# First units on the unnormalized input, weight sums on VectorE, and a longer load time in the scheduler: two layers of a hybrid decoder trunk

## The chip, the cores and the metric

The kernel runs on one core of one Trainium2 chip. The metric is device microseconds (us) of one execution. Engines are named as the profile names them: PE (TensorE; PEld is its weight load), DVE (VectorE), ACT (ScalarE), POOL (GpSimd), SP (the engine that issues most transfers).

## The reference

One sequence of 1024 positions, width 1024, two layers, all in f32. Each layer is a mixer and a squared-ReLU MLP, both behind an RMSNorm whose result is scaled and shifted by columns computed from a conditioning vector c. Here is what matters of it:

```python
mod = c_act @ ada_w[layer] + ada_b[layer]          # c_act = silu(c); 6 x 1024 columns
sh_m, sc_m, gt_m, sh_f, sc_f, gt_f = jnp.split(mod, 6, axis=-1)
h = rmsnorm(x, norm_mix_w[layer]) * (1 + sc_m) + sh_m
y = even_mixer(h, ...) if layer % 2 == 0 else odd_mixer(h, ...)
x = x + gt_m * y
h = rmsnorm(x, norm_mlp_w[layer]) * (1 + sc_f) + sh_f
x = x + gt_f * (jnp.square(jax.nn.relu(h @ w1)) @ w2)
# at the end: rmsnorm(x, final_norm_w)

# even_mixer: proj = h @ w_in, split into xr, yr, q, k, v, g (8 heads' worth of columns);
# xr: causal depthwise conv of width 4, then a gated linear recurrence (RG-LRU) times gelu(yr);
# q, k, v: rotary, chunkwise retention, group norm, times silu(g); both concatenated @ w_out
```

## The kernel before, in words

**Arithmetic.** Activations lie with features on the 128 partitions and half of the sequence, f = 0 or 1, in 512 columns. A dense product of two f32 matrices is made as three products of parts: each factor is split into a high part (a rounded copy, made by ACT) and a low part (the rest, made by a subtraction, mostly on DVE), and hi·hi, hi·lo and lo·hi are added up in PSUM (`mm3`). A *unit* is one 128-column block of a weight matrix: it takes 24 matmuls of 128x512 for each half, 48 in all. `operand` splits an activation, `split` a raw weight (loaded by SP as 512 KB into a `raw` slot).

**Order.** The program doesn't run in the order of its text. A `Recorder` collects every operation with an assumed duration, and `place()` schedules them all by simulation: of the operations that are ready, an engine takes the one with the smallest priority, which is its place in the text plus a bias (`with bias(...)`; BIG is larger than the program, LATER is 300 places). Slots come from pools: `heap` (73 slots of 128x512), `raw` (4), `w` (6), `pad` (4), and in PSUM `dps` (3) and `psum` (5). For a transfer the simulation adds bytes/380 ns to the time at which the transfers before it are through, and then 2000 ns until it has landed. What comes out is a fixed order for each engine and each queue; on the chip, every engine runs its list in that order and waits with semaphores.

**Start.** `csil`, the silu of c on all partitions, and `ccol`, the same as columns, come first. For each of 8 chunks j of the width, the shift `mod[:, j]` is a product on PE of `ada0[j]` with `ccol` (stationary a column of `ccol`, moving 128 columns of `ada0`, which gives a row that ACT copies and PE transposes to a column), and the scale `mod[:, 8+j]` is made by DVE from `ada[j]` and `csil`, and becomes `wsc[:, j]`. x's half 0 is loaded, its inverse root mean square `rs0` found by PE column sums (`rstd_half`), x multiplied by it (`scaled`), and `first_operand` makes the operand `x*rs0*wsc + mod`. Half 1 follows, its seven sums of squares on POOL. The first LEAD = 3 units then run together: their matmuls for f = 0, then those for f = 1 (f = 1 into the pool `psum`). Before, these are x0, x1 and q0 in `EVEN_ORDER` (x: input of the recurrence, y its gate, q, k, v, g of the retention); the low parts of their weights are made on POOL. `lru_in`, through `pad_in`, takes an x unit out of PSUM and convolves it.

**Then** 24 units of the even mixer in all, 16 units of the output projection (`out_proj`, whose 8 results per half are each added to x on DVE; after the last of a half a column sum on PE opens the norm), the MLP of layer 0, odd mixer, output projection, MLP of layer 1, final norm. Both products of an MLP are made by Strassen's scheme in Winograd's form: seven products P1 to P7 for each of 16 groups, 112 *steps* of 12 matmuls in the up half and 112 in the down half. Its weight operands need sums of blocks of the raw weights. Some are made by the transfer itself (`dma_add`: an accumulating transfer issued by POOL), two per group in each half by POOL's `tensor_tensor`: in the up half `x += P1` and `P2 += x` (`up_factor`), in the down half `a11 += x` and `a12 += a11` (`down_factor`); 128 over both layers. `W_LOADS` gives the step of the down half at which each weight block is asked for. `ada_some` asks for 512 KB of scale or gate weights that DVE multiplies with `csil` (tile names `raw<-raw,blk`); in the down half of layer 0 it is called at every fourth step. `last_adds` puts the last products of the down half into x.

## Time and profile before

| | us |
|---|---|
| median of 3 executions | 2349.3 |
| lowest and highest | 2345.51, 2351.92 |
| the profiled execution's own time | 2352.24 |
| its span | 2350.5 |
| mean granted TensorE clock, share of full speed | 0.991 |

The span is the time from the first to the last record of the profiled execution; 1.7 us of its own time lie around it. The profile is of one execution, so its rows add up to its own time, which is 3 us above the median. The kernel has about these stages: the start to 79 us, even mixer and output projection to 412, up half of layer 0 to 788, its down half to 1090, odd mixer and its output projection behind that, the same two halves for layer 1, and the final norm up to 2350.

### The profile page before, as it was taken

The numbers are of one execution on the slowest core, as the hardware profiler recorded it, in microseconds if no ns is written. First come the engines' busy times: TensorE is split into PE (matmuls) and PEld (weight loads), VectorE is DVE, ScalarE is ACT, GpSimd is POOL, SyncE is SP. The second block draws the span as 40 slices with busy tenths as digits, with TensorE's granted clock in tenths as the row PEclk, the third lists the DMA queues.
The fourth block names the chain that finished last, engine by engine and source line by source line (L and its number), as shares of the span: only waits on it lengthen the run. The fifth ranks groups of instructions, "written<-read, shape, count | busy, mean of one in ns | idle before, by whom it ended". The sixth has DMA issues, their size and how long they took to land.

```text
span 2350.5 us, 31521 instructions
## 1 busy us (share of the span) xinstructions
PE 2285.3 (97%) x10906; PEld 1871.1 (80%) x10906; DVE 1701.7 (72%) x2702; ACT 1275.0 (54%) x2377; POOL 513.5 (22%) x602
## 2 busy tenths in 40 slices
PE   7999999899999999999999999999999999999998
PEld 4787888678878778887787887888878888788886
DVE  7997667896555786887976687566687555676776
ACT  6787453565545544445755574656465555544444
POOL 3000000022221230500073426430022222140500
PEclk9999999999999999999999999999999999999999
DMA  8253338757664997753212122244358665896752
GB/s 290 90 135 117 117 120 283 246 157 219 192 180 156 311 346 244 211 189 117 73 39 77 48 57 68 59 141 141 128 154 238 194 188 159 265 312 193 185 161 94
DMA packets 199076, 393.35 MB, mean 167 GB/s; under 512 B 30146, under 2 KB 40962, under 8 KB 198916
## 3 DMA queue, kind: packets, MB, share of 16 engines
q1 hardware_dynamic: 180484, 357.78, 45.5%
q0 software_dynamic: 18432, 33.56, 8.8%
q8 instruction: 85, 1.39, 0.2%
q14 instruction: 75, 0.61, 0.1%
HBM read 308.91 MB, written 82.35 MB: 166 GB/s over the span
## 4 chain that ended last, share of the span: by engine, by line
PE 73%; issue 7%; DMA 7%; DVE 6%; ACT 5%; POOL 1%; SPq 0%; POOLq 0%; DVEq 0%; ACTq 0%
PE dps L342 39%; PE psum L342 35%; ACT heap L342 4%; DVE heap L342 4%; DMA raw<-in_dram 3%; DMA heap<-in_dram 1%; DMA h_spill<-heap 1%; DVE w L342 1%; ACT w L342 1%; POOL pad L342 1%; DVE raw L342 1%; DMA heap<-h_spill 1%; POOL raw L342 0%; POOL heap L342 0%; ACT L342 0%
## 5 line engine op out<-in xcount | busy, mean ns | idle before, releaser
L342 PE MATMUL dps<-heap,w 128*128 128x512 f32 x5016 | 1246.2, 396 | 14.9 <-DVE heap L342 8.7
L342 PEld LDWEIGHTS dps<-heap,w 128*128 128x128 f32 x5016 | 928.0, 189 | 211.0 <-ACT heap L342 10.6
L342 PE MATMUL psum<-heap,w 128*128 128x512 f32 x3816 | 899.7, 392 | 14.7 <-DVE blk L342 5.8
L342 PEld LDWEIGHTS psum<-heap,w 128*128 128x128 f32 x3816 | 718.9, 189 | 173.2 <-ACT heap L342 10.1
L342 ACT ACTIVATE heap<-heap 128x512 f32<-128x512 f32 (+2 forms) x1055 | 619.9, 609 | 258.6 <-DVE heap L342 200.5
L342 DVE TENSOR_TENSOR heap<-heap,heap 128x512 f32<-128x512 f32 (+1 forms) x799 | 580.2, 750 | 79.9 <-ACT heap L342 75.1
L342 ACT ACTIVATE w<-heap 128x512 fp32r<-128x512 f32 x224 | 140.6, 630 | 276.3 <-PE psum L342 219.9
L342 ACT ACTIVATE w<-raw 128x512 fp32r<-128x512 f32 (+1 forms) x248 | 192.2, 778 | 175.0 <-PE dps L342 93.6
L342 DVE TENSOR_TENSOR w<-raw,w 128x512 fp32r<-128x512 f32 (+1 forms) x213 | 192.9, 910 | 75.1 <-ACT w L342 69.6
L342 DVE TENSOR_TENSOR w<-heap,w 128x512 fp32r<-128x512 f32 x192 | 159.5, 836 | 97.1 <-ACT w L342 96.6
L342 POOL DMA_DIRECT2D raw<-in_dram x32 | 27.9, 873 | 718.5 <-DMA x_spill<-heap 297.3
L342 POOL TENSOR_TENSOR blk<-blk,blk 32x31 f32<-32x31 f32 (+15 forms) x248 | 173.9, 701 | 38.6 <-DMA blk<-n_full 11.5
L342 POOL TENSOR_TENSOR heap<-heap,heap 128x512 f32<-128x512 f32 x74 | 114.4, 1557 | 201.6 <-ACT heap L342 103.5
L342 ACT ACTIVATE heap<-psum 128x512 f32<-128x512 f32 (+6 forms) x189 | 89.3, 480 | 81.3 <-PE psum L342 80.4
L342 PE MATMUL psum<-heap,heap 128*128 128x128 f32 (+4 forms) x1064 | 130.5, 264 | 2.5 <-DVE heap L342 2.2
L342 PEld LDWEIGHTS psum<-heap,heap 128*128 128x128 f32 (+2 forms) x1064 | 113.1, 169 | 23.6 <-DVE heap L342 5.0
L342 DVE SCALAR_TENSOR_TENSOR raw<-raw,blk 128x1024 f32<-128x1024 f32 x80 | 98.8, 1237 | 30.2 <-DMA raw<-in_dram 29.8
L342 POOL DMA_DIRECT2D heap<-in_dram x64 | 59.8, 979 | 268.9 <-DVE heap L342 137.4
L342 DVE TENSOR_TENSOR w<-pad,w 128x512 fp32r<-128x512 f32 x64 | 58.3, 910 | 75.3 <-ACT w L342 75.2
L342 ACT ACTIVATE w<-pad 128x512 fp32r<-128x512 f32 x64 | 40.4, 632 | 126.0 <-POOL pad L342 71.4
L342 DVE TENSOR_TENSOR heap<-psum,heap 128x512 f32<-128x512 f32 x89 | 61.0, 686 | 48.2 <-PE psum L342 39.5
L342 ACT ACTIVATE heap<-dps 128x512 f32<-128x512 f32 (+1 forms) x134 | 77.5, 585 | 24.0 <-PE dps L342 13.7
(180 smaller groups left out, 1384.8 us busy)
## 6 DMA issues: line engine op xcount, KB each, us to landing
raw<-in_dram SPq DMA_DIRECT2D x232, 512.0 KB, 4.1
heap<-in_dram SPq DMA_DIRECT2D x226, 256.0 KB, 5.6
h_spill<-heap SPq DMA_DIRECT2D x224, 256.0 KB, 4.4
heap<-h_spill SPq DMA_DIRECT2D x224, 256.0 KB, 5.2
heap<-in_dram POOLq DMA_DIRECT2D x64, 256.0 KB, 6.8
x_spill<-heap SPq DMA_DIRECT2D x48, 256.0 KB, 3.1
heap<-x_spill SPq DMA_DIRECT2D x48, 256.0 KB, 5.4
pad<-in_dram SPq DMA_DIRECT2D x32, 256.0 KB, 2.5
```

The source lines that it names most:

```text
L342: op.call(*a, **k)
```

## The change

Five parts.

1. **Scheduler.** The transfer rate goes from 380 to 360 bytes per ns, and the time until a transfer has landed from 2000 ns to 3500 (issued by SP) or 5500 (issued by POOL). These numbers are only used to choose the order.
2. **Start.** x's half 0 is loaded chunk by chunk, each followed by its two scale weights. The operand of the lead units for f = 0 becomes `plain`, the split of x*wsc, without `rs0` and without the shift. What is missing is put in where the unit leaves PSUM: `pad_in` multiplies by `rs0` (a product along the columns) and adds `lead_bias`, a column per unit: the product of its raw weights with the shift, 24 matmuls with a single moving column, for which the three raw weights are held. The lead units become x0, x1, x2, which all leave through `pad_in`. f = 1 and all later units use the full operand as before. The shift is made with `ada0` as stationary factor and one column of `ccol` as moving one, which gives a column directly. The lead weights' low parts, and half 1's seven sums, go from POOL to DVE.
3. **Weight sums.** The 128 sums go from POOL to DVE.
4. **Loads of the MLP.** `W_LOADS`: in the down half x is asked for 8 steps earlier, a12 one, a21 six, a22 two. The scale and gate loads in the down half of layer 0 go from steps 2, 6, 10, ... to every third step from step 34 on.
5. `last_adds` gets the bias LATER.

The core of the diff:

```diff
-                    dma_free = max(dma_free, now) + op.bytes / 380.0
-                    op.end = dma_free + 2000.0
+                    dma_free = max(dma_free, now) + op.bytes / 360.0
+                    op.end = dma_free + (5500.0 if e == "POOL" else 3500.0)
...
-              "x0 x1 l2 q0 k0 v0 x2 x3 l2 q1 k1 v1 y0 y1 q2 k2 v2 y2 q3 k3 v3 y3 g0 g1 g2 g3".split()]
+              "x0 x1 x2 l2 q0 k0 v0 x3 l2 q1 k1 v1 y0 y1 q2 k2 v2 y2 q3 k3 v3 y3 g0 g1 g2 g3".split()]
...
-W_LOADS = {(i + n * j, name): j for i, n, name in ((-8, 1, "a11"), (0, 1, "a12"), (1, 2, "x"), (10, 2, "a21"), (24, 1, "a22"))
+W_LOADS = {(i + n * j, name): j for i, n, name in ((-8, 1, "a11"), (-7, 2, "x"), (-1, 1, "a12"), (4, 2, "a21"), (22, 1, "a22"))
...
-            split(hi, lo, raw, (), G if i < LEAD else V)
+            split(hi, lo, raw)
+            if i < LEAD:
+                lead_raw.append(raw)
...
             if kind == "P6":
-                G.tensor_tensor(pw["x"], pw["x"], pw["P1"], ALU.add)
+                V.tensor_tensor(pw["x"], pw["x"], pw["P1"], ALU.add)
...
         def last_adds(f, ks):
-            for k in ks:
-                add_to(f, k, shared[k % 4], f == 1 and k < 4)
+            with bias(LATER):
+                for k in ks:
+                    add_to(f, k, shared[k % 4], f == 1 and k < 4)
...
-            if l == 0 and n % 4 == 2:
+            if l == 0 and n >= 32 and n % 3 == 1:
                 ada_some(1, [marks[-1]])
...
+    plain = []
     for j in range(KC):
+        xh[0].append(ht("x"))
+        dma(xh[0][j], xT[j, :, 0:HT])
+        if 0 < j <= LEAD:
+            with bias(2 * BIG):
+                push()
...
+        w = wsc[:, j:j + 1]
+        V.scalar_tensor_tensor(w, mod[:, 8 + j:9 + j], 1.0, cc("nmix", j), ALU.add, ALU.mult)
+        hi, lo = hsplit_tiles()
+        act(hi, xh[0][j], AF.Copy, scale=w)
+        V.scalar_tensor_tensor(lo, xh[0][j], w, hi.bitcast(F32), ALU.mult, ALU.subtract)
+        plain.append((hi, lo))
+    xh[1] = load_half(xT, 1)
+    scaled(1, rstd_half(xh[1]))
+    rs0 = rstd_half(xh[0])
+    hh = [[], []]
+    pb = pmt()
+    for j in range(KC):
+        for q in range(2):
+            a = ht("ada")
+            dma(a, ada0[j][:, q * HT:(q + 1) * HT])
+            for k in range(4):
+                T.matmul(pb[:, j:j + 1], a[:, k * P:(k + 1) * P], ccol[:, 4 * q + k:4 * q + k + 1],
+                         start=(q == 0 and k == 0), stop=(q == 1 and k == 3))
+        V.tensor_tensor(mod[:, j:j + 1], pb[:, j:j + 1], cc("ada_b", j), ALU.add)
+        hh[1].append(first_operand(1, j))
+    lead_bias = small("lead_bias", [LEAD])
+    for u, raw in enumerate(lead_raw):
+        for k in range(KC):
+            T.matmul(pb[:, 8 + u:9 + u], raw[:, k * P:(k + 1) * P], mod[:, k:k + 1], start=(k == 0), stop=(k == KC - 1))
+    V.tensor_copy(lead_bias, pb[:, 8:8 + LEAD])
+    scaled(0, rs0)
+    for j in range(KC):
+        hh[0].append(first_operand(0, j))
...
     def pad_in(key, f, ps, b=None):
-        act(raw[:, 3:], ps, AF.Copy)
+        if b is None:
+            act(raw[:, 3:], ps, AF.Copy)
+        else:
+            V.tensor_tensor(raw[:, 3:], ps, rs0, ALU.mult)
+            act(raw[:, 3:], raw[:, 3:], AF.Identity, bias=b)
...
-    first = dense(hh, LEAD, pmt)
+    first = dense([plain, hh[1]], LEAD, pmt)
```

How the scheduler places it, at three places. Each row is an instruction: the helper's line, the operation, out<-in by tile names (pool and number), its shape, and how many alike follow each other.

**PE at the start of the program**, right behind the eight products that make `csil`. Before (`ccol` is the stationary column of the shift, `ones_r` the column sum of squares, `ident` the transpose of the row):

```order
L342 MATMUL psum_305<-s_301,ones_f 128x128
L342 MATMUL psum_334<-heap_168,ccol 1x128 x4
L342 MATMUL psum_334<-heap_170,ccol 1x128 x4
L342 MATMUL psum_349<-heap_340,ones_r 128x512
L342 MATMUL psum_334<-ident,s_351 128x1
L342 MATMUL psum_349<-heap_345,ones_r 128x512
L342 MATMUL psum_361<-heap_178,ccol 1x128 x4
L342 MATMUL psum_361<-heap_180,ccol 1x128 x4
L342 MATMUL psum_383<-heap_186,ccol 1x128
L342 MATMUL psum_361<-ident,s_379 128x1
L342 MATMUL psum_383<-heap_186,ccol 1x128 x3
L342 MATMUL psum_383<-heap_188,ccol 1x128 x4
L342 MATMUL dps_404<-heap_398,w_331 128x512
```

After:

```order
L342 MATMUL psum_301<-s_298,ones_f 128x128
L342 MATMUL dps_338<-heap_332,w_314 128x512
L342 MATMUL dps_342<-heap_332,w_325 128x512
L342 MATMUL dps_338<-heap_344,w_314 128x512
L342 MATMUL dps_338<-heap_332,w_319 128x512
L342 MATMUL dps_338<-heap_336,w_314 128x512
L342 MATMUL dps_338<-heap_346,w_314 128x512
L342 MATMUL dps_338<-heap_336,w_319 128x512
L342 MATMUL dps_342<-heap_344,w_325 128x512
```

The shift products, the column sum and the transposes stood ahead of the first dense matmul (`dps<-heap,w`); now the dense matmuls of the lead units follow at once.

**PE at the end of the first half of the output projection of layer 0.** The dense rows are units of half f = 1, and `psum<-heap,ones_r` is the column sum for f = 0, which waits for the last addition to x. Before:

```order
L342 MATMUL dps_3777<-heap_3404,w_3690 128x512
L342 MATMUL dps_3777<-heap_3306,w_3707 128x512
L342 MATMUL dps_3777<-heap_3392,w_3690 128x512
L342 MATMUL dps_3777<-heap_3479,w_3690 128x512
L342 MATMUL psum_3816<-heap_3804,ones_r 128x512
L342 MATMUL dps_3777<-heap_3392,w_3707 128x512
L342 MATMUL dps_3777<-heap_3494,w_3690 128x512
L342 MATMUL dps_3777<-heap_3506,w_3690 128x512
L342 MATMUL psum_3816<-heap_3811,ones_r 128x512
```

After:

```order
L342 MATMUL dps_3840<-heap_3284,w_3771 128x512
L342 MATMUL dps_3840<-heap_3330,w_3771 128x512
L342 MATMUL dps_3840<-heap_3284,w_3781 128x512
L342 MATMUL psum_3847<-heap_3835,ones_r 128x512
L342 MATMUL dps_3840<-heap_3297,w_3771 128x512
L342 MATMUL dps_3840<-heap_3343,w_3771 128x512
L342 MATMUL dps_3840<-heap_3297,w_3781 128x512
L342 MATMUL dps_3840<-heap_3301,w_3771 128x512
L342 MATMUL dps_3840<-heap_3381,w_3771 128x512
L342 MATMUL dps_3840<-heap_3301,w_3781 128x512
L342 MATMUL dps_3840<-heap_3310,w_3771 128x512
L342 MATMUL dps_3840<-heap_3387,w_3771 128x512
```

Before, 20 dense matmuls stand between the last unit of f = 0 and the first column sum; after, 27, and the second column sum follows 12 rows behind the first in place of 3.

**The weight sums at the start of the up half of layer 0.** Before, on POOL, between the issues of transfers (`DMA`; `pad` holds x, `raw` holds P1 and P2):

```order
L342 DMA pad_1697<-in_dram 128x512
L342 DMA raw_4145<-in_dram 128x512
L342 TENSOR_TENSOR pad_1395<-pad_1395,raw_4139 128x512
L342 DMA raw_4245<-in_dram 128x512
L342 TENSOR_TENSOR raw_4139<-raw_4139,pad_1395 128x512
L342 DMA pad_4312<-in_dram 128x512
L342 TENSOR_TENSOR pad_1485<-pad_1485,raw_4234 128x512
```

After, on DVE, between the operand splits (`w<-pad,w` is the low part of a weight factor, `heap<-heap,wsc,heap` the norm's product for an activation):

```order
L342 TENSOR_TENSOR w_4260<-raw_4219,w_4260 128x512
L342 SCALAR_TENSOR_TENSOR heap_4281<-heap_3457,wsc,heap_4265 128x512
L342 TENSOR_TENSOR w_4278<-pad_1332,w_4278 128x512
L342 SCALAR_TENSOR_TENSOR heap_4292<-heap_3466,wsc,heap_4265 128x512
L342 TENSOR_TENSOR pad_1332<-pad_1332,raw_4166 128x512
L342 SCALAR_TENSOR_TENSOR heap_4302<-heap_3459,wsc,heap_4265 128x512
L342 TENSOR_TENSOR raw_4166<-raw_4166,pad_1332 128x512
L342 TENSOR_TENSOR w_4304<-pad_1332,w_4304 128x512
```

Both sums now stand in DVE's order, in which a wait for their inputs holds back what stands behind them.

## Rows read from the trace of the kernel before

**Rows 1.** The profile page, part 1: busy time of each engine, its share of the span, and its instructions.

```profile
PE 2285.3 (97%) x10906; PEld 1871.1 (80%) x10906; DVE 1701.7 (72%) x2702; ACT 1275.0 (54%) x2377; POOL 513.5 (22%) x602
```

**Rows 2.** The timeline of PE, at eight places. Columns: start and length in us, engine, line, operation, out<-in, partitions by columns, shape, count; in brackets the idle time just before it and what released it. Nearly everything runs through one helper line, so the line says nothing here.

```profile
419.65 0.79 PE L342 MATMUL psum<-heap,ones_r 128*128 128x512 f32 x1 [7.44 <-ACT heap L342]
...
494.87 0.80 PE L342 MATMUL psum<-heap,w 128*128 128x512 f32 x1 [2.08 <-ACT heap L342]
...
531.38 2.79 PE L342 MATMUL psum<-heap,w 128*128 128x512 f32 x11 [1.42 <-ACT heap L342]
...
804.83 1.58 PE L342 MATMUL psum<-heap,w 128*128 128x512 f32 x4 [2.88 <-DVE blk L342]
...
839.57 2.93 PE L342 MATMUL dps<-heap,w 128*128 128x512 f32 x6 [2.61 <-DVE heap L342]
...
1744.27 0.96 PE L342 MATMUL psum<-heap,w 128*128 128x512 f32 x3 [1.38 <-DVE heap L342]
...
1777.36 2.81 PE L342 MATMUL psum<-heap,w 128*128 128x512 f32 x11 [1.09 <-ACT heap L342]
...
2050.25 3.35 PE L342 MATMUL psum<-heap,w 128*128 128x512 f32 x9 [2.74 <-DVE blk L342]
```

**Rows 3.** Busy time in windows: the stretch in us, its length, then for PE, PE's weight loads, DVE, ACT and POOL the busy us with (instructions), the granted TensorE clock as a share of full speed, the DMA share and GB/s.

```profile
50.00:100.00 50.00, 49.17 (x206) 37.45 (x204) 46.99 (x102) 39.24 (x63) 0.00 (x0) 1.00 0.22 72
...
150.00:200.00 50.00, 48.31 (x241) 39.38 (x240) 44.19 (x77) 42.41 (x82) 1.74 (x2) 1.00 0.46 127
...
200.00:250.00 50.00, 49.58 (x257) 41.39 (x256) 35.70 (x77) 26.30 (x71) 0.00 (x0) 1.00 0.37 116
...
420.00:425.00 5.00, 5.00 (x16) 3.95 (x16) 3.94 (x7) 2.79 (x4) 0.00 (x0) 0.69 0.90 290
...
495.00:500.00 5.00, 4.65 (x10) 3.21 (x11) 5.00 (x9) 3.04 (x5) 0.88 (x1) 0.50 0.47 90
```

**Rows 4.** The timeline of PE from 55 to 90 us: the first matmuls of the lead units' second half, and the fourth unit's 42 first ones (they write to the pool dps).

```profile
60.69 0.84 PE L342 MATMUL psum<-heap,w 128*128 128x512 f32 x3
...
78.97 9.68 PE L342 MATMUL dps<-heap,w 128*128 128x512 f32 x42
```

**Rows 5.** The timeline of DVE (first three) and of POOL, which is GpSimd (last two), from 0 to 65 us.

```profile
6.26 1.66 DVE L342 TENSOR_SCALAR s<-ident,ccol 128x128 f32<-128x128 f32 x8
...
28.96 1.70 DVE L342 SCALAR_TENSOR_TENSOR heap<-heap,blk 128x512 f32<-128x512 f32 x1
...
55.76 8.57 DVE L342 TENSOR_TENSOR heap<-heap,heap 128x512 f32<-128x512 f32 x14 [1.14 <-ACT heap L342]
...
13.53 2.46 POOL L342 TENSOR_TENSOR w<-raw,w 128x1024 fp32r<-128x1024 f32 x1 [11.66 <-ACT w L342]
...
28.54 11.46 POOL L342 TENSOR_TENSOR heap<-heap,heap 128x512 f32<-128x512 f32 x7 [1.93 <-ACT heap L342]
```

**Rows 6.** The DMA view from 0 to 60 us: GB/s in 40 slices of 1.5 us.

```profile
GB/s 0 145 269 276 272 333 421 395 399 404 388 389 386 400 393 393 373 386 391 378 382 385 385 384 388 386 389 374 244 69 109 295 391 364 21 5 11 0 0 0
```

**Rows 7.** PE's instructions grouped by line and form: shapes, count, then busy us, mean ns of one (the ends of pipelined ones overlap, so busy divided by count is the pace), and the idle time before them.

```profile
L342 PE MATMUL psum<-heap,ccol 128*1 128x128 f32 x128 | 17.9, 293 | 5.7 <-DMA heap<-in_dram 5.7
...
L342 PE MATMUL psum<-heap,heap 128*128 128x64 f32 x128 | 16.2, 268 | 0.0
...
L342 PE MATMUL psum<-heap,heap 128*32 128x32 f32 x256 | 11.5, 202 | 0.0
```

**Rows 8.** The timeline of DVE from 405 to 440 us (first three), where raw<-raw,blk is the product of a gate weight and heap<-dps,mod,heap the addition of one projection unit to x; and from the DMA view of 350 to 430 us the issues of one kind, with KB each and the median us from issue to landing.

```profile
411.85 0.74 DVE L342 SCALAR_TENSOR_TENSOR heap<-dps,mod,heap 128x512 f32<-128x512 f32 x1
...
415.30 1.23 DVE L342 SCALAR_TENSOR_TENSOR raw<-raw,blk 128x1024 f32<-128x1024 f32 x1 [0.97 <-DMA raw<-in_dram]
...
416.45 0.75 DVE L342 SCALAR_TENSOR_TENSOR heap<-dps,mod,heap 128x512 f32<-128x512 f32 x1
...
raw<-in_dram SPq DMA_DIRECT2D x31, 512.0 KB, 4.7
```

**Rows 9.** The weight sums: from the timeline of POOL and of ACT around 490 us and of POOL around 527 us, then one form of POOL and one of DVE over the whole span (count, busy us, mean ns, idle before and its releasers).

```profile
487.99 2.86 POOL L342 TENSOR_TENSOR pad<-pad,raw 128x512 f32<-128x512 f32 x1 [5.03 <-DVE w L342]
...
490.88 0.63 ACT L342 ACTIVATE w<-pad 128x512 fp32r<-128x512 f32 x1 [1.03 <-POOL pad L342]
...
526.60 0.89 POOL L342 DMA_DIRECT2D raw<-in_dram  x1 [6.72 <-DMA h_spill<-heap]
...
L342 POOL TENSOR_TENSOR heap<-heap,heap 128x512 f32<-128x512 f32 x74 | 114.4, 1557 | 201.6 <-ACT heap L342 103.5 <-DMA heap<-in_dram 43.3 <-DVE w L342 34.6
...
L342 DVE TENSOR_TENSOR heap<-heap,heap 128x512 f32<-128x512 f32 x431 | 303.9, 719 | 52.7 <-ACT heap L342 48.3
```

**Rows 10.** The passage from up half to down half in layer 0: from the timeline of DVE one low part of a weight factor, from that of POOL two sums beside it, and from the DMA view of 780 to 880 us the total and the issues of two kinds.

```profile
834.00 3.38 DVE L342 TENSOR_TENSOR w<-heap,w 128x512 fp32r<-128x512 f32 x1
...
833.99 2.83 POOL L342 TENSOR_TENSOR heap<-heap,heap 128x512 f32<-128x512 f32 x2
...
DMA packets 17244, 34.11 MB, mean 341 GB/s; under 512 B 1914, under 2 KB 1914, under 8 KB 17236
...
heap<-in_dram SPq DMA_DIRECT2D x32, 256.0 KB, 7.8
...
heap<-in_dram POOLq DMA_DIRECT2D x16, 256.0 KB, 7.0
```

40 lines of the change are left out of this document (9 added, 31 removed).

## Prediction, made before the changed kernel was run

> **What bounds the kernel now.** I read the page first: of a span of 2350.5 us TensorE (PE) is busy 2285.3, 97% [rows 1]. Only its idle time, 65 us, and time at a reduced clock can be won; no edit takes dense matmuls away. Next I listed where PE waits. It waits at the start, where no unit can run before the norm and the modulation are there. After that it loses single stretches of 1 to 7 us, which [rows 2] show with what released them: the end of the output projection, the first steps of each MLP's up half, and the passage to its down half. Each stretch has a tail. The windows behind two of them [rows 3] show a granted clock of 0.69 and 0.50 and 16 and 10 matmuls in 5 us; at full speed 42 take 9.68 us [rows 4], 0.23 each, so 22 fit. The tail costs 6 x 0.23 = 1.4 us, and 2.8 in the second case.
>
> VectorE (DVE) is the other engine to watch: busy 72% overall, but 44.19 to 46.99 us of 50 in the even mixer up to 200 us, and 35.70 behind that [rows 1, 3]. What lands on it early can reach PE; later it has 14 us in 50 to spare.
>
> **A. The start.** Before, the three lead units run their second half from 60.69 us and the fourth unit begins at 78.97 [rows 4]. After, the first half needs only the scale of its chunk. Three sides bound it.
>
> *Loads.* The stage moves the same bytes. The x half, the scale weights and three raw weights (7.5 MB) stand first; by the rates of [rows 6] 7.7 MB are there at some 23.5 us, and 13.9 MB, with shift weights and second half, at some 42.
>
> *DVE.* I counted its operations in the order of after up to the last operand of the second half: 67 of 512 wide, 3 of 1024, 26 small. At 0.61 (14 in 8.57 us, [rows 5]), 1.22 (twice the width) and 0.07 each that is 46.4 us; from 7.9 us, when the eight ident products end [rows 5], and with 2.7 us for the inverse root in ACT, the last operand stands at 57 us. Nine matmuls follow it, and the fourth unit could begin near 63 us.
>
> *PE.* From 28 us (loads of the first half, then the last chunk) it has 16.6 us of second-half matmuls, some 6 of column sums, gaps and setup, and 88 calls with one moving column: 64 for the shift, 24 for the bias of the lead units. The trace has none of these. Before, the 64 shift products took 17.9 us [rows 7]. A call is two instructions; the nearest rows are 16.2/128 = 0.127 us for 128 stationary and 64 moving columns and 11.5/256 = 0.045 for 32 and 32 [rows 7], so 88 calls cost 7.9 to 22.4 us. I take 22.4, the row with equal stationary width: the fourth unit then begins at 73 us. The Trainium skill ("TensorE: Matmul & The Clock Gate", "LDWEIGHTS (loading the stationary operand)") prices a weight load by its columns, 128/1.2 = 107 ns; by that the calls would cost 18.8 us, an estimate, and the unit begin near 69. No run here shows this form.
>
> So PE leads by 6 to 16 us. But DVE now also makes the three low parts and seven sums that GpSimd made (2.46 us there for the first low part, 11.46 for the seven sums, [rows 5]), and eight products for the lead units: 18 x 0.61 + 3 x 1.22 = 14.6 us more by the end of this stage. It gets back what contention took: beside the seven sums on GpSimd its own operations were stretched (one of 0.61 took 1.70); about 10 us in all by such rows. DVE is thus 4 to 5 us later than before where the stage ends, while PE is 6 to 16 us earlier, and behind it both are nearly full. Bounds: -16 (all of PE's lead stays), +4 (DVE's delay reaches PE). I take **-8**, near the middle, as PE was the fuller of the two at 50 to 150 us.
>
> **B. End of the output projection.** PE stands 7.44 us at 419.65, the longest gap after the start, then 1.4 us of half clock [rows 2, 3]. The path: the last addition to x came at 416.45, behind a gate-weight product that waited for its load until 415.30, while its unit had long ended (the one before was added at 411.85) [rows 8]. In-order DVE waits on a load, and PE on DVE. The order assumed such a load to land 2 us after its transfer; the median was 4.7 for 512 KB, of which the move itself at the 390 GB/s of [rows 6] is 1.3 [rows 8]. With 3.5 us assumed, the orders show 27 dense rows between the last unit of the half and the column sum in place of 20: 7 x 0.23 = 1.6 us more cover, and the addition no longer stands behind a late load. Bounds 0 to -8.8; I take **-6**.
>
> *A rule against this.* The Trainium skill ("DMA: Bandwidth & Descriptors", "Anatomy of one DMA — SWDGE (gpsimd) path") gives about 2.0 us fixed and bytes/436e9 of transfer, 3.2 us for 512 KB: by it the old constant was right, no wait came from the order, and B and D below are 0. The trace disagrees (4.7, and 7.8 in the busy passage, [rows 8, 10]); it is a rival.
>
> **C. Weight sums off GpSimd.** 128 sums move to DVE: up to 2.86 us there where PE then stands, against a mean of 0.72 on DVE [rows 9]. At 494.87 PE waited behind ACT, ACT behind the sum (487.99 to 490.85) [rows 2, 9]; 531.38 follows from a sum queued behind a GpSimd DMA issue that waited until 526.60 [rows 9]. The same four places in both layers: 2.08 + 2.8 (half clock) + 1.42 + 1.38 + 1.09 = 8.8 us [rows 2]. The x loads also start earlier: load 7.8 plus accumulation 7.0 needs 15 us; by the matmuls between them in the order the lead was 11 to 14 us and is 27 to 35. Work for DVE: 128 x 0.72 = 92 us, 46 a layer. An MLP has 224 steps of 12 matmuls, 618 us at 0.23; with DVE idle 28% of the time that leaves 170 us for 46, and DVE loses the stretching by GpSimd (mean 0.72 against 0.61 clean, [rows 5, 9]). So this work costs nothing, hidden behind the matmuls; without that cover it would cost up to 92. Bounds -10 (with small gaps beside these) to -3 (the half-clock tail alone); I take **-7**.
>
> **D. Passage to the down half.** 2.88 + 2.61 + 2.74 us and a half-clock tail of 1.4 each, 12.4 us [rows 2, 3]. Here transfers run at 341 GB/s on the mean, loads take 7.8 us, and a DVE operation beside two GpSimd sums took 3.38 us [rows 10]. No sums on GpSimd removes the stretching; gate-weight loads of layer 0 now begin at step 32 of the down half, which takes 512 KB loads out of the crowded passage; the last additions go 300 places later. Against it: weights for the down half are asked earlier in the same crowd, and DVE does the sums. Bounds -10 to +6; I take **-4**.
>
> **Sum.** -8 - 6 - 7 - 4 = -25, with 4 us either way for all other reshuffling. The profiled execution took 2352.2 us, 3 above the median 2349.3; I set the sum against the median: 2349.3 - 25 = **2324, say 2325**. A difference under 0.3% (7 us) can't be told from none.
>
> **Rivals.** *R1, slower: the sums wait on DVE.* GpSimd's sums waited 43.3 us for loads [rows 9]. On DVE, in order, such a wait holds back all operand splits behind it, and so PE. If all of it reached PE with four half-clock tails: 2349.3 - (25 - 4, D gone) + 43.3 + 5.6 = 2377. It decides from about half (21 us) on. For it: B is just this, DVE waiting for a load. Against: the lead doubled. *R2: DVE eats the start.* Its delay of 4 to 5 us stands instead of PE's lead: A = +4, total 2349 - 13 = 2336. For it: DVE 94% busy at 50 to 100 us; against: PE's lead is larger. *R3: the longer load time lifts no stall*, as in the rule above: B = D = 0, A and C stay: 2349 - 15 = 2334. For it: transfers were moved, not shortened. *R2 and R3 together*: A = +4, C = -7: 2346, no change. *Larger*: all bounds near their good ends (-16, -8.8, -10, -10): 2349 - 44 = 2305.
>
> **How the numbers follow.** Forecast 0.42, R2 0.14, R3 0.13, R2 with R3 0.10, R1 0.10, larger 0.11. Range 2306 to 2350: from the larger case to no change, leaving out R1 and half of the larger. Faster: 0.42 + 0.14 + 0.13 + 0.11 = 0.80, less 0.02 for scatter of R2: 0.78. Same: 0.10 + 0.02 = 0.12. Slower: 0.10.
>
> **What would show it.** A: the fourth unit's first matmul near 70 us (63 to 73); 79 or later says R2, with DVE at 49 of 50 to 200 us. The 88 calls between 8 and 22 us. B: the gap at the end of the first output projection under 2 us. C: no PE gap released by a sum in the first 40 us of either up half; if DVE waits for loads into pad or heap buffers before a sum, over 5 us in all, it is R1. D: gaps at the passage under 5 us in all; 10 or more says R3. What would make it wrong above all: that DVE, at 94% early, sets the pace where I took PE's.

## The result, and the profile after

The changed kernel takes 2322.1 us in the median of 5 executions (2319.6 to 2330.1), the kernel before, in 5 executions of its own, 2351.9 (2345.5 to 2355.4). The ratio is 0.9884, with an interval from 0.9860 to 0.9908. Forecast were 2325 us within 2306 to 2350. The time is right, but its parts are not: the start lost what the prediction let it win, and the rest won about twice what was forecast.

Part 1 of the page after, and its line of the granted TensorE clock in 40 slices of 58 us, in tenths:

```profile
PE 2292.6 (98%) x10946; PEld 1895.7 (81%) x10946; DVE 1700.1 (73%) x2852; ACT 1283.2 (55%) x2377; POOL 311.2 (13%) x464
...
PEclk8799999999999999999999999999999999999999
```

DVE made 150 instructions more than in [rows 1] and is busy as long as before (1700.1 against 1701.7 us), and POOL lost 202 us. In the clock line the second slice, 58 to 116 us, stands at 7 tenths; in the kernel before, every slice of this line is a 9.

The windows, with the columns of [rows 3]:

```profile
50.00:100.00 50.00, 50.00 (x189) 42.93 (x188) 19.37 (x39) 22.01 (x35) 0.00 (x0) 0.60 0.17 53
100.00:150.00 50.00, 49.88 (x223) 40.57 (x222) 49.04 (x106) 30.62 (x52) 0.00 (x0) 1.00 0.37 115
400.00:450.00 50.00, 49.90 (x221) 40.81 (x220) 44.57 (x66) 19.82 (x27) 0.00 (x0) 1.00 0.95 331
450.00:500.00 50.00, 49.87 (x219) 40.55 (x218) 48.09 (x77) 37.43 (x66) 3.45 (x4) 1.00 0.71 213
800.00:850.00 50.00, 49.81 (x220) 40.94 (x219) 37.43 (x60) 22.93 (x40) 9.01 (x11) 1.00 1.07 335
2050.00:2100.00 50.00, 49.81 (x220) 40.92 (x219) 35.02 (x56) 22.40 (x39) 3.48 (x4) 1.00 0.88 293
```

From 50 to 100 us PE is busy all the time, at a granted clock of 0.60, and DVE only 19.37 us of 50, where it was 46.99 [rows 3]. The stretches with the gaps of [rows 2] are full now: 49.90 and 49.87 us of 50 around the first output projection and the first up steps, 49.81 in both passages, all at clock 1.00. So there is one stage with a loss, and it is the one in which the prediction expected a gain.

The same is seen by stage if one counts dense matmuls (those that read a weight slot, 8864 in every kernel here) and compares when the n-th begins in the two profiled executions. Each column ends at the n in its head and is what that stage gained (minus) or lost (plus) against the profiled execution of before, in us. The names are rough: "down half 0" takes in the first part of the odd mixer, and in the kernel before the output projection ends at n = 1536, at 460.8 us, not at 412 as the list of stages ahead of the prediction has it.

| kernel | start, n to 144 | even mixer, 1152 | first output projection, 1536 | up half 0, 2592 | passage 0, 3264 | down half 0, 4608 | odd mixer, 6000 | up half 1, 7400 | passage 1, 8000 | end, 8700 | sum |
|---|---|---|---|---|---|---|---|---|---|---|---|
| changed kernel | +19.8 | -0.7 | -8.9 | -11.1 | -8.9 | +0.4 | +0.1 | -7.4 | -4.1 | -0.3 | -21.1 |
| e1 old start | +1.9 | -1.4 | -9.3 | -11.7 | -8.8 | +0.4 | -0.4 | -7.3 | -4.1 | -0.3 | -41.1 |
| e2 row products | -1.7 | -0.9 | -9.4 | -11.3 | -8.8 | +0.2 | 0.0 | -7.4 | -4.1 | -0.3 | -43.8 |
| e3 wide columns | +5.8 | -0.7 | -8.6 | -10.7 | -8.9 | +0.3 | +0.1 | -7.4 | -4.1 | -0.3 | -34.3 |
| e4 old load time | +19.1 | +3.9 | -2.1 | -12.1 | -2.4 | +1.1 | -0.5 | -7.4 | +1.9 | -0.3 | +1.1 |
| e5 load time only | +2.1 | -1.0 | -9.3 | -6.4 | -1.7 | +5.6 | -0.4 | +0.2 | +5.0 | +7.0 | +1.0 |
| e6 sums only | +1.8 | +0.6 | -0.1 | -11.7 | -4.7 | -0.4 | +0.9 | -7.3 | +2.1 | -0.3 | -18.9 |
| e7 sums on GpSimd | +9.0 | -0.7 | -9.4 | -8.7 | -5.9 | +6.6 | -0.4 | 0.0 | +0.6 | +2.9 | -6.1 |
| e8 old load steps | +9.0 | -0.7 | -9.3 | -10.2 | -4.8 | +2.9 | +0.1 | -7.4 | -4.6 | -0.3 | -25.1 |
| e9 load time and sums | +0.9 | -1.0 | -9.3 | -9.7 | -4.4 | +1.4 | -2.0 | -7.3 | -4.6 | -0.3 | -36.5 |
| e10 idle GpSimd sums | -1.4 | -1.3 | -9.4 | -5.4 | +2.2 | +15.5 | +0.7 | +4.7 | +7.6 | +12.2 | +25.3 |
| e11 longer load time | -1.9 | -1.0 | -5.4 | -12.8 | -8.7 | +3.9 | +14.9 | -7.3 | -4.0 | -0.3 | -22.4 |
| e12 start only | +9.6 | +4.3 | -1.8 | +3.2 | -4.2 | +1.1 | -0.4 | +3.3 | -3.1 | 0.0 | +12.1 |

The profiled execution of the changed kernel (2330.1 us) is the slowest of its five, and its start the worst one seen (+19.8; +19.1 in e4, which has the same start, and +9.0 in e7 and e8, which have the same start and scheduler numbers). Behind the start it agrees with e1 to e3, which differ from it in the start alone, within 0.8 us in every column.

**The start.** PE's timeline after, where the first two rows are dense matmuls of the lead units' first half, `psum<-ccol,heap` are the shift products with one moving column and `psum<-mod,raw` those for the bias:

```profile
13.90 1.22 PE L342 MATMUL dps<-heap,w 128*128 128x512 f32 x2 [4.21 <-ACT heap L342]
15.66 16.62 PE L342 MATMUL dps<-heap,w 128*128 128x512 f32 x60 [0.54 <-DVE heap L342]
32.12 0.95 PE L342 MATMUL psum<-ccol,heap 128*128 128x1 f32 x8
...
42.58 3.58 PE L342 MATMUL psum<-ccol,heap 128*128 128x1 f32 x16 [0.25 <-DVE mod L342]
...
50.73 3.40 PE L342 MATMUL psum<-ccol,heap 128*128 128x1 f32 x16
...
57.13 3.41 PE L342 MATMUL psum<-ccol,heap 128*128 128x1 f32 x16
...
75.05 10.23 PE L342 MATMUL psum<-mod,raw 128*128 128x1 f32 x48
85.14 6.03 PE L342 MATMUL psum<-heap,w 128*128 128x512 f32 x16
...
98.79 13.40 PE L342 MATMUL dps<-heap,w 128*128 128x512 f32 x57
```

and windows of 5 us there:

```profile
40.00:45.00 5.00, 4.75 (x31) 4.58 (x29) 2.63 (x6) 4.65 (x7) 0.00 (x0) 0.69 0.52 143
45.00:50.00 5.00, 4.24 (x13) 3.14 (x13) 5.00 (x10) 3.87 (x9) 0.00 (x0) 0.50 0.06 14
...
80.00:85.00 5.00, 5.00 (x25) 5.00 (x25) 0.00 (x0) 0.60 (x2) 0.00 (x0) 0.50 0.57 192
...
90.00:95.00 5.00, 5.00 (x17) 2.45 (x16) 2.72 (x3) 3.05 (x4) 0.00 (x0) 1.00 0.32 97
```

The fourth unit begins at 98.79 us, in [rows 4] at 78.97. Up to 42 us eight one-column instructions take 0.95 us, 0.12 each. The clock then falls to 0.50, the lower of its two levels (1.2 in place of 2.4 GHz): from 42 to 85 us, while PE does one-column products by 16 and a few dense matmuls in turn and stands idle almost nowhere (busy 4.24 of 5 us from 45 to 50, all the time from 50 on), 16 of them take 3.4 us, 0.21 each. It is granted in full again behind the 16 dense matmuls that begin at 85.14 us. By the records PE is busy 5.00 of 5 us through most of this; only the clock column shows that it runs at half speed. The Trainium skill ("TensorE: Matmul & The Clock Gate", "LDWEIGHTS (loading the stationary operand)") gives 107 ns for loading 128 columns; at the full clock the trace agrees as far as the pace goes (0.12 us per instruction, load and product together).

### The profile page after: what moved, and what is told of

The parts are those of the page before. It is cut to its first block, busy times and chain, and to the rows that moved or that the text cites. A ratio compares the mean times of both kernels' runs of the same rounds, so it can differ in the third digit from the quotient of the medians.

```text
span 2328.3 us, 31553 instructions
## 1 busy us (share of the span) xinstructions
PE 2292.6 (98%) x10946; PEld 1895.7 (81%) x10946; DVE 1700.1 (73%) x2852; ACT 1283.2 (55%) x2377; POOL 311.2 (13%) x464
## 4 chain that ended last, share of the span: by engine, by line
PE 83%; DVE 6%; issue 6%; ACT 3%; DMA 1%; POOL 0%; SPq 0%; POOLq 0%; DVEq 0%; ACTq 0%
PE psum L342 43%; PE dps L342 39%; DVE heap L342 4%; ACT heap L342 2%; DVE w L342 1%; DMA raw<-in_dram 1%; DVE raw L342 1%; ACT w L342 1%; DMA heap<-in_dram 0%; ACT L342 0%; POOL heap L342 0%; SPq L342 0%; ACT pad L342 0%; DVE blk L342 0%; POOLq L1943 0%
## 5 line engine op out<-in xcount | busy, mean ns | idle before, releaser
L342 DVE TENSOR_TENSOR heap<-heap,heap 128x512 fp32r<-128x512 f32 (+1 forms) x870 | 580.5, 691 | 65.8 <-ACT heap L342 60.3
L342 DVE TENSOR_TENSOR w<-heap,w 128x512 fp32r<-128x512 f32 x192 | 132.2, 688 | 121.2 <-ACT w L342 120.8
L342 POOL TENSOR_TENSOR blk<-blk,blk 32x31 f32<-32x31 f32 (+15 forms) x248 | 168.8, 681 | 33.6 <-issue 9.2
L342 ACT ACTIVATE heap<-psum 128x512 f32<-128x512 f32 (+4 forms) x187 | 88.5, 480 | 84.8 <-PE psum L342 82.9
L342 ACT ACTIVATE heap<-dps 128x512 f32<-128x512 f32 (+1 forms) x136 | 78.9, 586 | 18.1 <-PE dps L342 11.7
L342 DVE SCALAR_TENSOR_TENSOR heap<-pad,col,heap 128x512 f32<-128x512 f32 x96 | 78.1, 819 | 0.3
L342 DVE TENSOR_TENSOR w<-pad,w 128x512 fp32r<-128x512 f32 x64 | 44.1, 689 | 39.3 <-ACT w L342 39.2
```

The source lines that it names most:

```text
L342: op.call(*a, **k)
```

## The experiments

**e1: the old start in the changed kernel.** The hunks of part 2 of the change are taken out, all others stay:

```diff
-    first = dense([plain, hh[1]], LEAD, pmt)
+    first = dense(hh, LEAD, pmt)
...
-              "x0 x1 x2 l2 q0 k0 v0 x3 l2 q1 k1 v1 y0 y1 q2 k2 v2 y2 q3 k3 v3 y3 g0 g1 g2 g3".split()]
+              "x0 x1 l2 q0 k0 v0 x2 x3 l2 q1 k1 v1 y0 y1 q2 k2 v2 y2 q3 k3 v3 y3 g0 g1 g2 g3".split()]
```

> The changed kernel with the start of before (norm and shift first, x0 x1 q0 as lead units); scheduler numbers, sums, loads and the late additions stay changed. In the changed kernel's trace the fourth unit begins at 98.79 us in place of 78.97, and the granted clock is 0.50 from 45 to 85 us. Theory one (the new start costs some 20 us, and the rest of the change gained some 45): fourth unit near 79 us, time near 2322 - 20 = 2302 us, no long stretch at half clock. Rival (the later start is given back behind it, since VectorE with 19 of 50 us busy from 50 to 100 us gains slack): 2322 us, within 5.

Measured: 2312.5 us (2310.4 to 2317.0), ratio to before 0.9842 [0.9821, 0.9864]; the fourth unit begins at 80.91 us. That is 9.6 us less than the changed kernel: theory one in direction, at half its size, which had been taken from the one profiled execution with the worst start. The rest of the change is thus worth 37 us (2349.7 to 2312.5).

**e2: the same start, products in row form.** The column is the stationary factor, 128 weight columns move:

```diff
-                T.matmul(pb[:, j:j + 1], a[:, k * P:(k + 1) * P], ccol[:, 4 * q + k:4 * q + k + 1],
+                T.matmul(pm[0:1, 0:P], ccol[:, 4 * q + k:4 * q + k + 1], a[:, k * P:(k + 1) * P],
                          start=(q == 0 and k == 0), stop=(q == 1 and k == 3))
+        act(row[0:1], pm[0:1, 0:P], AF.Copy)
+        T.transpose(pm[:, P:P + 1], row[0:1], ident[0:1, 0:1])
...
-            T.matmul(pb[:, 8 + u:9 + u], raw[:, k * P:(k + 1) * P], mod[:, k:k + 1], start=(k == 0), stop=(k == KC - 1))
+            T.matmul(pm[0:1, 0:P], mod[:, k:k + 1], raw[:, k * P:(k + 1) * P], start=(k == 0), stop=(k == KC - 1))
```

> The changed kernel; only the 64 shift products and the 24 bias products change their form: the single column is the stationary factor and 128 weight columns move, the row that results is copied by ScalarE and transposed by PE, as the shift was before. Theory one (the one-column products themselves hold the clock at half): granted clock back near 1 from 50 us on, fourth unit at 70 to 80 us, time 2297 to 2307. Rival (the operands' chain PE, VectorE, ScalarE, PE sets the pace of the start, whatever the form): fourth unit past 90 us, time 2317 to 2327.

Measured: 2308.6 us (2307.4 to 2309.6), ratio 0.9819 [0.9803, 0.9835], the fastest kernel of the study and 13.5 us under the changed one. Its timeline of PE and its windows:

```profile
43.54 4.09 PE L342 MATMUL psum<-heap,ccol 128*1 128x128 f32 x36
...
77.24 13.99 PE L342 MATMUL dps<-heap,w 128*128 128x512 f32 x61
```

```profile
40.00:45.00 5.00, 5.00 (x43) 3.41 (x43) 3.13 (x6) 4.77 (x8) 0.00 (x0) 1.00 0.53 155
45.00:50.00 5.00, 5.00 (x45) 3.45 (x43) 4.77 (x13) 4.68 (x12) 0.00 (x0) 1.00 0.09 19
50.00:55.00 5.00, 5.00 (x44) 3.76 (x43) 5.00 (x10) 5.00 (x10) 0.00 (x0) 1.00 0.00 0
50.00:100.00 50.00, 49.79 (x237) 38.60 (x236) 47.33 (x104) 37.67 (x65) 0.00 (x0) 1.00 0.30 95
```

36 instructions of the row form take 4.09 us (0.114 each, as long as a one-column one at the full clock), the clock stays at 1.00, DVE is busy 47.33 us of 50, and the fourth unit begins at 77.24. So it is the form of the products and what the clock does under it, not the chain of operands, which is longer here by a copy and a transpose. The order on PE changed with the form, though: nearly all products of this kind now run ahead of the second half's dense matmuls and not in turn with them. No run changes that order alone, so its part in the clock stays open. Against the old start (e1) the new idea itself is then worth 3.9 us by medians; every execution of e2 is below every one of e1, though the intervals of the two ratios overlap.

**e3: 32 equal moving columns for the shift products.**

```diff
-                T.matmul(pb[:, j:j + 1], a[:, k * P:(k + 1) * P], ccol[:, 4 * q + k:4 * q + k + 1],
+                T.matmul(pb[:, j * WD:(j + 1) * WD], a[:, k * P:(k + 1) * P], cwide[:, (4 * q + k) * WD:(4 * q + k + 1) * WD],
```

> The changed kernel, but the 64 shift products move 32 equal columns in place of one, with the same stationary loads and the same number of instructions (8 small copies on VectorE make the columns). It tells what in these products goes with the low clock. If the number of moving columns matters: the clock rises earlier than at 85 us, fourth unit at 75 to 92 us, time 2300 to 2315. If the number of instructions and stationary loads alone matters: clock 0.50 up to 85 us as before, fourth unit at 98 to 100 us, time 2320 to 2326.

Measured: 2320.0 us (2316.8 to 2323.5), fourth unit at 84.81 in the profiled execution (2316.8). Its windows:

```profile
50.00:55.00 5.00, 5.00 (x18) 4.45 (x19) 1.96 (x4) 2.33 (x4) 0.00 (x0) 0.50 0.00 0
55.00:60.00 5.00, 5.00 (x38) 4.62 (x36) 1.96 (x4) 2.56 (x4) 0.00 (x0) 0.99 0.01 3
60.00:65.00 5.00, 5.00 (x36) 4.54 (x35) 2.57 (x6) 2.88 (x5) 0.00 (x0) 1.00 0.00 0
...
70.00:75.00 5.00, 5.00 (x16) 4.23 (x17) 3.53 (x10) 1.43 (x3) 0.00 (x0) 0.50 0.60 199
```

The two expectations split: the profile seems to answer to the first (84.81; clock at 0.99 and 1.00 from 55 to 65 us, in the middle of the wide products), the median lies at the edge of the second's range and 2.1 us from the changed kernel's. But the return of the clock is not the wide columns' doing. It comes as well with one column: in e12 (below), and likewise in e7 and e8, the clock is 1.00 from 55 to 65 us. The lines of e12, where 16 one-column products take 1.84 us at 55.76:

```profile
55.76 1.84 PE L342 MATMUL psum<-ccol,heap 128*128 128x1 f32 x16
...
55.00:60.00 5.00, 5.00 (x36) 4.54 (x35) 3.15 (x6) 3.63 (x7) 0.00 (x0) 1.00 0.01 3
60.00:65.00 5.00, 5.00 (x35) 4.60 (x36) 2.14 (x6) 2.84 (x5) 0.00 (x0) 1.00 0.00 0
```

In all of these the clock falls a second time behind 65 us, in the 48 bias products, which have one column in e3 too (64.83 to 71.4). So e3 doesn't tell whether the number of moving columns matters. Executions with the same one-column products differ, and the changed kernel's profile, at half clock from 42 to 90 us without a break, is the long case.

**e12: the new start alone on the kernel before.**

```diff
-    first = dense(hh, LEAD, pmt)
+    first = dense([plain, hh[1]], LEAD, pmt)
...
```

> The kernel before with the new start alone (first units on the unnormalized input, one-column products, x0 x1 x2 as lead units); old numbers, sums on GpSimd, old loads. The rest of the change can hide or share nothing here. Theory (the one-column products cost more clock than the earlier units win): fourth unit past 88 us, granted clock 0.50 in most of 45 to 85 us, time 2353 to 2366, slower than before by 4 to 16 us. Rival (as the prediction had it: 8 us faster): 2338 to 2346. Rival two (the rest of the kernel takes the delay up, since VectorE is ahead by then): 2347 to 2352.

Measured: 2371.4 us (2361.9 to 2374.8, 6 executions), ratio 1.0091 [1.0071, 1.0111]: 22.7 us slower, more than any expectation. The profiled execution is again a better one (2363.3, fourth unit at 88.55):

```profile
40.00:90.00 50.00, 49.39 (x229) 42.02 (x229) 27.99 (x53) 31.78 (x50) 0.00 (x0) 0.74 0.23 69
```

By an estimate from the mean clock, half clock costs 0.26 x 50 = 13 us there; in the changed kernel's profile 0.40 x 50 = 20 from 50 to 100 us alone. The length of the slow stretch differs between executions, and so does the time (2361.9 to 2374.8). By the stages this execution loses 9.6 at the start, 4.3 in the even mixer, as e4 does with the same two parts, and 6.5 in the up halves; why the start makes the old up halves worse was not followed. That the loss is 22.7 us alone and 9.6 in the changed kernel is thus explained in part only.

**e4: the old load time in the changed kernel.**

```diff
-                    dma_free = max(dma_free, now) + op.bytes / 360.0
-                    op.end = dma_free + (5500.0 if e == "POOL" else 3500.0)
+                    dma_free = max(dma_free, now) + op.bytes / 380.0
+                    op.end = dma_free + 2000.0
```

> The changed kernel with the scheduler's old transfer numbers (380 bytes per ns, 2000 ns). Theory (they removed the waits for loads): the gap at the end of the first output projection (7.44 us before, under 0.3 after) comes back with 5 to 8 us, and 3 to 10 us come back at the passage to the down half; time 2322 + 8 to 18 = 2330 to 2340. Rival (the waits went because sums and gate loads moved, not by these numbers): 2317 to 2327.

Measured: 2345.4 us (10 executions), ratio 0.9990 [0.9970, 1.0010]: 23 us of the gain are gone. PE's timeline:

```profile
440.51 0.79 PE L342 MATMUL psum<-heap,ones_r 128*128 128x512 f32 x1 [5.36 <-ACT heap L342]
```

```profile
815.42 2.90 PE L342 MATMUL psum<-heap,w 128*128 128x512 f32 x6 [4.77 <-DVE blk L342]
```

```profile
2051.66 1.62 PE L342 MATMUL psum<-heap,w 128*128 128x512 f32 x3 [4.63 <-DVE blk L342]
```

The gap at the output projection is back with 5.36 us, and both passages are with 4.77 and 4.63: the theory, and larger than it said. Against the changed kernel the stages lose 6.8 at the output projection, 6.5 and 6.0 at the passages, and 4.6 in the even mixer, which it had not named.

**e5: the load time alone, on the kernel before.** The two lines of e4 the other way.

> The kernel before with only the scheduler's transfer numbers changed (360 bytes per ns; 3500 and 5500 ns). Putting the old numbers back into the changed kernel cost 23 us. Theory (the numbers by themselves let the order ask for loads and place the operations behind them where they land): the gap of 7.44 us at the first output projection under 1.5 us, those at the passages to the down halves (2.88, 2.61, 2.74) under 1.5 us in sum per layer, the half-clock tails gone with them; the gaps behind GpSimd's sums (494.87, 531.38) stay; time 2322 to 2332. Rival (they help only where the sums have left GpSimd and the loads are asked earlier): 2338 to 2350.

Measured: 2350.8 us (10 executions), ratio 0.9997 [0.9983, 1.0012]: nothing. The theory failed, and the stage table says how: the output projection gains its 9.3 us and the first up half 6.4, and the down halves lose 5.6, 5.0 and 7.0. One such place, on DVE, POOL and PE:

```profile
2194.96 4.42 DVE L342 TENSOR_TENSOR heap<-heap,heap 128x512 fp32r<-128x512 f32 x1
2199.30 3.42 DVE L342 TENSOR_TENSOR w<-heap,w 128x512 fp32r<-128x512 f32 x1
```

```profile
2195.04 1.61 POOL L342 TENSOR_TENSOR heap<-heap,heap 128x512 f32<-128x512 f32 x1
...
2196.88 1.93 POOL L342 TENSOR_TENSOR heap<-heap,heap 128x512 f32<-128x512 f32 x1
...
2198.90 3.25 POOL L342 TENSOR_TENSOR heap<-heap,heap 128x512 f32<-128x512 f32 x2
```

```profile
2203.46 2.90 PE L342 MATMUL psum<-heap,w 128*128 128x512 f32 x6 [4.95 <-DVE blk L342]
```

GpSimd makes four sums with hardly a pause, and beside them one subtraction on DVE takes 4.42 us and the next 3.42, in place of 0.61 [rows 5]; PE stands 4.95.

**e6: the sums alone, on the kernel before.** Four lines of this kind:

```diff
-                G.tensor_tensor(pw["x"], pw["x"], pw["P1"], ALU.add)
+                V.tensor_tensor(pw["x"], pw["x"], pw["P1"], ALU.add)
```

> The kernel before with only the 128 sums moved from GpSimd to VectorE; old scheduler numbers, old load steps, old start. Theory (the sums held up PE at the first steps of each up half, and only there): gaps at 494.87, 531.38, 1744.27, 1777.36 gone, the 7.44 us at the output projection stays; at the passage to the down half VectorE now waits in order for late loads, 3 to 8 us for each layer; time 2335 to 2347. Rival one (the sums on GpSimd stretched VectorE and so made the passages slow, too): passages under 2 us, time 2322 to 2332. Rival two (VectorE's waits for loads reach PE in full): 2355 or more.

Measured: 2326.5 us (2323.1 to 2334.1), ratio 0.9883 [0.9860, 0.9906]: as much as the whole change, and rival one's number. By the stages it is in part the theory's: the gaps of the first up steps are gone, and the up halves (-11.7 and -7.3) hold all of the profiled execution's 18.9, twice the 8.8 that the prediction counted in their gaps and tails. That execution is the slowest of four, and it doesn't show where the rest of the median's 26.7 us lies. At the passages the gaps are 1.97 us in layer 0 and 2.00 and 2.00 in layer 1, in part under rival one's 2 us and in part the theory's 3 to 8. Loads end 6.3 us of DVE's idle time in the form that now holds the down halves' sums (`heap<-heap,heap`), which is what R1 expects, and the kernel is faster all the same. The output projection still stands:

```profile
421.41 0.79 PE L342 MATMUL psum<-heap,ones_r 128*128 128x512 f32 x1 [6.23 <-ACT heap L342]
```

**e7: the sums back on GpSimd in the changed kernel.** The four lines of e6 the other way.

> The changed kernel with the 128 sums back on GpSimd; new numbers, new load steps and new start stay. Theory (sums on GpSimd cost some 9 to 12 us of gaps and tails at the first steps of the up halves): 2330 to 2336, with gaps released by ACT behind a GpSimd sum near 490 to 535 and 1720 to 1760 us. Rival (the longer load time and the earlier loads give the sums enough lead wherever they run): 2318 to 2326.

Measured: 2352.3 us (10 executions), ratio 1.0001 [0.9985, 1.0017]: 30 us lost, three times the expected amount. By the profiled execution, the fastest of the ten, the up halves lose 2.4 and 7.4 us against the changed kernel, which is the theory; passage 0 (3.0), down half 0 (6.2), passage 1 (4.7) and the last down steps (3.2) lose 17.1 more, which it did not hold.

**e8: the old load steps in the changed kernel.**

```diff
-W_LOADS = {(i + n * j, name): j for i, n, name in ((-8, 1, "a11"), (-7, 2, "x"), (-1, 1, "a12"), (4, 2, "a21"), (22, 1, "a22"))
+W_LOADS = {(i + n * j, name): j for i, n, name in ((-8, 1, "a11"), (0, 1, "a12"), (1, 2, "x"), (10, 2, "a21"), (24, 1, "a22"))
...
-            if l == 0 and n >= 32 and n % 3 == 1:
+            if l == 0 and n % 4 == 2:
```

> The changed kernel with the old steps for the weight loads of the down half, the old steps for its scale and gate loads, and the last additions without their later place. Theory (the passages were won by the scheduler's numbers, these steps add little): 2319 to 2327, gaps at the passages under 2 us in sum. Rival (the steps took the gate loads out of the crowded passage, and without them it stalls again): 3 to 8 us of gaps near 800 and 2030 us with half-clock tails, time 2328 to 2336.

Measured: 2327.4 us (2323.2 to 2336.5), ratio 0.9896 [0.9868, 0.9925]; that is at the border of the two forecasts, 5.3 us over the changed kernel by medians, and the intervals overlap. In the stage table passage 0 gives back 4.1 us and down half 0 2.5, passage 1 nothing: in place of gaps near 800 and 2030 as the rival had it there is one of 2.20 us at 860. The load steps, the steps of the gate loads and the later place of `last_adds` went back together and are not parted.

**e9: load time and sums together, without the new start and the new load steps.** The diffs of e5 and e6.

> The kernel before with two parts of the change: the scheduler's transfer numbers and the 128 sums on VectorE; old start, old load steps. Alone, the numbers gave 0 and the sums 25 us. Theory (the numbers take the waits for loads away everywhere, but with sums on GpSimd what they win is lost again in the down halves, where GpSimd's sums come in clusters and hold back VectorE): 25 + 9 for the output projection + 2 to 6 for the passages, 2309 to 2317 us, no gap at the first output projection and gaps at 2200 us gone. Rival (the two win the same waits): 2321 to 2329.

Measured: 2321.8 us (2317.2 to 2322.7), ratio 0.9876 [0.9860, 0.9893]. By the time it is the rival's: 4.7 us under the sums alone, with overlapping intervals. By the stages it is the theory's: the output projection keeps its 9.3 us, the down halves lose nothing more, and the sum is -36.5 against -18.9; but the profiled execution here is the fastest of its four, and that of e6 the slowest. How much the two add to each other stays open between 5 and 18 us; that the load time's loss in the down halves goes where the sums leave GpSimd is seen in both e9 and e1. These two differ in parts 4 and 5 of the change alone: with the old start those are worth 9.3 us by medians (2321.8 to 2312.5), every execution of e1 below every one of e9.

**e10: sums on GpSimd that nobody waits for.** The kernel of e2, and behind each of the four sums a line like

```diff
                 V.tensor_tensor(pw["x"], pw["x"], pw["P1"], ALU.add)
+                G.tensor_tensor(ht("scr"), pw["x"], pw["P1"], ALU.add)
```

> The kernel of e2 (the changed kernel with the products in row form, 2308.6 us), and behind each of the 128 sums on VectorE a sum of the same inputs on GpSimd into a spare buffer that nobody reads: extra work that leaves the output as it is. It parts the two ways in which a sum on GpSimd can cost: that PE's operands wait for its result, or that VectorE's operations are stretched while it runs. If the waiting is the cost: 2307 to 2313. If the stretching is: 2320 to 2340, with VectorE's subtractions for weight factors back at 0.8 us and more in the mean (0.69 without).

Measured: 2376.7 us (2376.4 to 2378.3), ratio 1.0110 [1.0095, 1.0125]: 68 us slower than e2, though no result of GpSimd is read, and past the range of either case. DVE's subtractions for weight factors, in the kernel before, after, and here:

```profile
L342 DVE TENSOR_TENSOR w<-heap,w 128x512 fp32r<-128x512 f32 x192 | 159.5, 836 | 97.1 <-ACT w L342 96.6
```

```profile
L342 DVE TENSOR_TENSOR heap<-heap,heap 128x512 f32<-128x512 f32 x502 | 342.1, 695 | 50.1 <-ACT heap L342 45.1 <-PE psum L342 1.1
...
L342 DVE TENSOR_TENSOR w<-heap,w 128x512 fp32r<-128x512 f32 x192 | 132.2, 688 | 121.2 <-ACT w L342 120.8
...
L342 DVE SCALAR_TENSOR_TENSOR raw<-raw,blk 128x1024 f32<-128x1024 f32 x80 | 97.2, 1218 | 5.6 <-DMA raw<-in_dram 5.3
```

```profile
L342 DVE TENSOR_TENSOR w<-heap,w 128x512 fp32r<-128x512 f32 x192 | 152.3, 794 | 122.4 <-ACT w L342 121.8
```

```profile
953.98 4.73 PE L342 MATMUL psum<-heap,w 128*128 128x512 f32 x12 [7.51 <-DVE heap L342]
963.06 12.15 PE L342 MATMUL psum<-heap,w 128*128 128x512 f32 x43 [4.34 <-DVE blk L342]
```

836 ns, 688 ns, and 794 ns again: the sums on GpSimd stretch DVE's operations while they run, and that brings PE's gaps back, released by DVE. With the same 2854 instructions DVE is busy 1773.9 us in place of e2's 1701.2, while its idle time ended by transfers hardly grows (13.6 us after 10.0), so late loads are not the way. It is more than e7's 30 us; DVE still makes its own 128 sums here, each spare buffer takes a `heap` slot, and the inputs' slots stay taken until GpSimd has read them, so the size isn't that of the stretching alone; the kind is.

**e11: a still longer load time.** The kernel of e2 with

```diff
-                    op.end = dma_free + (5500.0 if e == "POOL" else 3500.0)
+                    op.end = dma_free + (7000.0 if e == "POOL" else 5000.0)
```

> The kernel of e2 with still longer transfer numbers in the scheduler (5000 ns for SP, 7000 ns for GpSimd, in place of 3500 and 5500). Theory (no wait for a load is left that ends on PE, so nothing is to be won; holding slots longer may cost a little): 2305 to 2314. Rival (waits for loads that landed later than 3.5 us are still in the small gaps): under 2303.

Measured: 2333.5 us (2329.4 to 2334.7): 25 us slower than e2, which neither expected. The up halves and passages keep their gain; 14.9 us go in the odd mixer, 4.0 at the output projection and 3.7 in down half 0. In the odd mixer there are gaps of this kind:

```profile
1504.01 0.49 PE L342 MATMUL psum<-s,heap 128*128 128x128 f32 x2 [2.19 <-DVE s L342]
1506.47 0.79 PE L342 MATMUL dps<-heap,w 128*128 128x512 f32 x1 [1.98 <-DVE heap L342]
```

They are released by DVE, in a stage of short dependent operations, and not by loads. At the first of them the short operation that PE waits for stands in DVE's order behind a weight split of 1.42 us, which itself waited 0.99 us for ACT; why the order puts it there was not followed further.

## Why the prediction was right and wrong

**Total.** 2325 was forecast and 2322.1 came, because misses of opposite sign cancel: A -8 against +9.6 measured (e1), and B, C and D -17 against -37. That the total was met is luck.

**A, the start: wrong in sign.** The loads were bounded well (143 GB/s from 40 to 45 us, 14 behind it: they end near 42). The step that failed is the one on PE: "I take 22.4 ... the fourth unit then begins at 73 us". At full clock 176 instructions of 0.12 are 21 us, and e2's take 21.0, so the price was right for the full clock; in the changed kernel's profile they took 33.3 us. That this form can hold the clock at half, for the dense matmuls beside it too, was in no term and in no bound, though [rows 3] showed that a tail at half clock doubles the time of what runs in it. A smaller miss stands beside it: PE was to be through with the first half's 72 matmuls at 28 us and had made 62 of them at 32.1, as it got its first operands from ACT and DVE at 13.90 and 15.66 us only (DVE is busy 10.00 us of 10 from 10 to 20), and 60 of them took 16.62 us from there. So e2's fourth unit, without the half clock, begins at 77.24 and not at 73, and the new start is worth 3.9 us there against e1, half of the 8. The time of 63 us for DVE's side has a gap in it as well: nine matmuls behind 57 us are 2 us, not 6. R2 named the mark (79 us or later) but the wrong cause: from 50 to 100 us DVE was idle most of the time (busy 19.37 of 50).

**B, the output projection: right in kind.** -6 forecast, -8.9 measured in the stage: the whole upper bound of 8.8. The last addition of the half comes at 429.49, 2.9 us after PE has begun the next half's first unit (426.6; before, the addition came at 416.45, 8.9 us after 407.5). PE runs through to the column sum and doesn't wait:

```profile
429.49 0.75 DVE L342 SCALAR_TENSOR_TENSOR heap<-dps,mod,heap 128x512 f32<-128x512 f32 x1
```

```profile
394.63 38.24 PE L342 MATMUL dps<-heap,w 128*128 128x512 f32 x168
432.71 0.48 PE L342 MATMUL psum<-heap,ones_r 128*128 128x512 f32 x1
```

e4 and e5 show that the scheduler's numbers do it, with the sums on either engine; its rate and its landing time were not parted. The loads have not become faster: 512 KB took 4.7 us before [rows 8], and in the same stretch after, with the columns of [rows 8]:

```profile
raw<-in_dram SPq DMA_DIRECT2D x29, 512.0 KB, 4.8
```

The order no longer counts on them. So R3 is out, and with it the use of the Trainium skill's fixed 2.0 us ("DMA: Bandwidth & Descriptors", "Anatomy of one DMA — SWDGE (gpsimd) path") as a price for when a load's result can be used here; that section is on transfers issued by GpSimd, and SP issues these. DVE's idle time before gate-weight products, 29.8 us on loads before, is 5.3 after (row above).

**C, the sums: mechanism half right, far too small.** -7 forecast; -11.1 and -7.4 in the up halves, and 27 to 30 us by medians for the sums as a whole (e6, e7). The step that failed is "So this work costs nothing, hidden behind the matmuls", with DVE losing the stretching as a mean (0.72 against 0.61): the term counted the gaps behind waited-for sums alone, and took from the stretching nothing for PE. DVE's total did come out even (1701.7 and 1700.1). But the stretching comes in bursts, where GpSimd makes several sums in a row, and there it is on PE's path (e5); e10 shows it without any wait for a result. The 14 us in 50 that DVE has to spare are an average and don't cover a burst like e5's, where two operations of 0.61 take 7.8 us.

**D, the passages: right in kind, -4 against -13.0.** Of this, sums and numbers together bring -4.4 and -4.6 (e9), parts 4 and 5 the other 4.1 of passage 0 (e8). Neither the numbers alone (-1.7, +5.0) nor the sums alone (-4.7, +2.1) do both passages.

**R1** fell: before the form on DVE that now holds the down halves' sums (`heap<-heap,heap`, row after e10) only ACT and PE end idle time, where loads ended 43.3 us of GpSimd's [rows 9]; the sums' inputs are early enough. **The range** held, but not for the reason given: B, C and D together went past the sum of their good ends (-28.8), A past its bad one (+4). Without A's loss e1 and e2 lie at 2312.5 and 2308.6, near the low end.
